# All gate and up pairs as seven-product jobs, with the norm's scale moved onto the gate

## The chip, the cores and the metric

The kernel runs on one core of one Trainium2 chip, as one launch. The metric is the device time of one execution in microseconds. The core's engines are named as in the profile: PE is TensorE's matmuls and PEld its weight loads, DVE is VectorE, ACT is ScalarE, POOL is GpSimd, SP is SyncE, which issues most of the DMA transfers. A name with a q (SPq, POOLq) is the queue of that engine.

## The reference, cut to what matters

A decoder of two layers computes one step for 512 prompt tokens and 32 sample tokens, 544 in all, in float32 with 1024 features. Each layer has a mixer (a short gated convolution in the first, retention with four heads in the second) and a gated feed-forward with 2816 hidden features:

```
x = x + mixer(rmsnorm(x, norm_mix))
x = x + (silu(h @ w_gate) * (h @ w_up)) @ w_down      with h = rmsnorm(x, norm_ffn)
rmsnorm(x, g) = x * rsqrt(mean(x*x over features) + 1e-6) * g
```

The scale `rsqrt(...)` is one number per token, the gain `g` one per feature. Since `h @ w` is linear, the scale of a token may be put on the result of the product instead of on its operand. That fact is used by both kernels, in different places.

## The kernel before, in words

Features lie on the 128 partitions and tokens along the free dimension. The residual x is eight tiles of 128 x 544 (x0 to x7). TensorE multiplies in a reduced float32 format, so each float32 operand is split into a high and a low part and each product is three matmuls: high by high, high by low, low by high. A matmul has 128 x 128 weights and 272 tokens, half of the 544. `split` (L184) makes the parts: ScalarE copies the high part (L185), VectorE subtracts it (L186). `split_adding` (L189) makes the low part in another way: ScalarE copies the negated high part and a DMA issued by GpSimd adds the source to it in memory (L193). Weights come as pieces of 128 x 1024 through three buffers (`wts`).

**The gate and up products.** The hidden features are 22 blocks of 128, taken as 11 pairs (m, m + 11). An ordinary pair takes 192 matmuls: a gate and an up piece for each of two blocks, each 8 feature tiles x 3 x 2 halves of the tokens (`project`, L164). A seven-product job does the gate (or the up) of a pair for both halves of the tokens as one 2 x 2 block product by seven multiplications in place of eight: 7 x 4 x 3 = 84 matmuls, so 168 for gate and up. It works on sums and differences: `weights7` (L407) makes those of the weights (four VectorE operations over 512 columns and four splits), `operands` (L397) those of x, once a layer, as seven operand tiles for each of four pairs of feature tiles (k, k + 4). The seven products accumulate in three PSUM banks; between products ScalarE copies a running sum out (a snapshot, L515) and VectorE adds it to others (L518). Class `Job` (L440) has the products as `begin`, `middle` and `end`; `run` (L490) puts the next job's beginning between the middle and the end of the one before.

**Before the change**, the first two pairs of each layer (`WHOLE = 2`) are ordinary ones (`whole_pairs`, L555). Their operands are x times the gain, split into `xh` and `xl` as the residual becomes final (`split_x`, L195); the norm's scale R goes onto their results. While they run, the sum of squares (`square_sum`, L205, with GpSimd adding, L215) becomes R (`rms_scale`: five one-column matmuls L244, a power on GpSimd L220, six small matmuls L224, a copy L256). Then `operand` (L546) makes the job operands as x times gain times R on VectorE. Jobs for the pairs 2 to 10 follow. After each three pairs `down` (L645) multiplies by w_down and adds to x (`residual`, L264).

**What stands ahead of the jobs.** In the first layer it is the convolution's output projection: eight blocks of 48 matmuls, one for each tile of x. In the second layer it is the last head's output projection (`out_project`, L1141): eight blocks of 24 matmuls, the first two interleaved.

**What sets the order.** The kernel is written with a tile framework that schedules the instructions itself: it orders each engine's queue from its own estimates of durations and inserts the waits. At run time each engine executes its queue strictly in that order. So the order in the text above is not always that on an engine.

## Time and profile before

| | us |
|---|---|
| runs shown | 1469.80, 1469.88, 1473.02 |
| their median | 1469.88 |
| the profiled execution, its own time | 1470.36 |
| its span in the profile | 1468.5 |
| TensorE busy in the span | 1457.3 |

The span runs from the first to the last recorded instruction of the profiled execution. Times in a timeline are from the start of the span. In a group's row stand the line, the engine, the operation, output and inputs by the program's names, the shape and the count; behind the bar the busy time and the mean duration of one in ns; and last the idle time of that engine ahead of them with what ended it. Matmuls overlap one another, so the sum of their durations is more than the time they take. In the rows of a stretch each engine's busy time is followed by its number of instructions.

### The profile page before, as it was taken

To read this page: it belongs to the slowest core of one execution; us is meant where nothing else is said; L and a number is where in the kernel's file an instruction comes from. 1 tells how busy PE (TensorE), PEld (TensorE's weight loads), DVE (VectorE), ACT (ScalarE), POOL (GpSimd) and SP (SyncE) were. 2 spreads that over 40 slices of the span, in tenths; PEclk is the share of its full clock that TensorE was granted. 3 is DMA by queue.
4 is the path that set the end of the run, shared out by engine and by line. 5 is a ranking of instruction groups with operands and counts; after the bars stand their busy time and mean duration, and the time that the engine had idled before them with its cause. 6 is when DMAs were issued, how large, how long until landed. Compare 5 with 4: busy or idle time off the path is not lost.

```text
span 1468.5 us, 26015 instructions
## 1 busy us (share of the span) xinstructions
PE 1457.3 (99%) x11016; PEld 1388.8 (95%) x11016; DVE 920.5 (63%) x1397; ACT 572.4 (39%) x821; POOL 84.3 (6%) x107
## 2 busy tenths in 40 slices
PE   9999999999999999999999999999999999999998
PEld 9999999999999999897987988898799999999997
DVE  6545439847748647648645934844759847748645
ACT  5222355625525434242142224114265625525424
POOL 0100220000000003000000000000030000000002
PEclk9999999999999999999999999999999999999999
DMA  6222274232322325336335613714564232332322
GB/s 226 86 87 87 89 179 109 91 100 90 102 94 87 101 65 181 116 115 232 100 115 173 202 49 121 264 42 143 173 158 108 91 105 87 104 92 93 101 65 83
DMA packets 69748, 172.83 MB, mean 118 GB/s; under 512 B 6512, under 2 KB 23792, under 8 KB 69632
## 3 DMA queue, kind: packets, MB, share of 16 engines
q1 hardware_dynamic: 66576, 162.01, 33.9%
q0 software_dynamic: 2192, 7.94, 3.3%
q8 instruction: 86, 1.41, 0.4%
q10 hardware_dynamic: 864, 1.22, 0.2%
q14 instruction: 30, 0.25, 0.1%
HBM read 149.97 MB, written 21.18 MB: 117 GB/s over the span
## 4 chain that ended last, share of the span: by engine, by line
PE 93%; DVE 4%; DMA 2%; POOL 1%; ACT 0%; issue 0%; DVEq 0%; POOLq 0%; ACTq 0%; SPq 0%
PE mm L172 41%; PE sm L458 26%; PE sm L172 13%; PE sm L906 2%; PE sm L907 2%; PE sm L908 2%; DMA S<-in_rets_dram 2%; DVE S L1138 1%; PE sm L160 1%; PE sm L162 1%; PE sm L161 1%; PE sm L1117 1%; PE mm L913 1%; DVE yn L1048 0%; DVE wl L186 0%
## 5 line engine op out<-in xcount | busy, mean ns | idle before, releaser
L185 ACT ACTIVATE wh<-w 128x1024 fp32r<-128x1024 f32 (+4 forms) x215 | 210.0, 980 | 448.2 <-PE mm L172 252.2
L186 DVE TENSOR_TENSOR wl<-w,wh 128x1024 fp32r<-128x1024 f32 (+4 forms) x215 | 243.1, 1134 | 44.3 <-ACT wh L185 40.9
L172 PE MATMUL mm<-xh,wh 128*128 128x272 f32 x1060 | 222.7, 291 | 0.0
L172 PE MATMUL mm<-xh,wl 128*128 128x272 f32 x1060 | 219.2, 289 | 0.0
L172 PE MATMUL mm<-xl,wh 128*128 128x272 f32 x1060 | 218.8, 288 | 0.0
L172 PEld LDWEIGHTS mm<-xh,wh 128*128 128x128 f32 x1060 | 166.5, 189 | 5.0 <-DVE wl L186 3.4
L458 PE MATMUL sm<-oh,wh 128*128 128x272 f32 x576 | 166.7, 289 | 0.0
L458 PE MATMUL sm<-oh,wl 128*128 128x272 f32 x576 | 166.6, 289 | 0.0
L172 PEld LDWEIGHTS mm<-xl,wh 128*128 128x128 f32 x1060 | 166.4, 189 | 0.0
L458 PE MATMUL sm<-ol,wh 128*128 128x272 f32 x576 | 166.3, 289 | 0.0
L172 PEld LDWEIGHTS mm<-xh,wl 128*128 128x128 f32 x1060 | 165.5, 189 | 0.4
L266 DVE TENSOR_TENSOR x<-x,mm 128x544 f32<-128x544 f32 x85 | 61.2, 720 | 144.8 <-PE mm L172 144.8
L458 PE MATMUL sm<-oh,l 128*128 128x272 f32 x432 | 124.9, 289 | 0.0
L458 PE MATMUL sm<-oh,h 128*128 128x272 f32 x432 | 124.8, 289 | 0.0
L458 PE MATMUL sm<-ol,h 128*128 128x272 f32 x432 | 124.8, 289 | 0.0
L458 PEld LDWEIGHTS sm<-oh,wh 128*128 128x128 f32 x576 | 108.7, 189 | 0.5 <-ACT u L515 0.4
L458 PEld LDWEIGHTS sm<-oh,wl 128*128 128x128 f32 x576 | 108.8, 189 | 0.0
L458 PEld LDWEIGHTS sm<-ol,wh 128*128 128x128 f32 x576 | 108.6, 188 | 0.0
L186 DVE TENSOR_TENSOR l<-w,h 128x1024 fp32r<-128x1024 f32 x72 | 68.8, 956 | 55.6 <-ACT h L185 55.4
L172 PE MATMUL mm<-xh,f 128*128 128x272 f32 x576 | 99.3, 288 | 0.0
L172 PE MATMUL sm<-xh,wh 128*128 128x272 f32 x412 | 88.4, 291 | 0.3 <-DVE rs L219 0.3
L172 PE MATMUL sm<-xh,wl 128*128 128x272 f32 x412 | 86.7, 288 | 0.0
(268 smaller groups left out, 2866.5 us busy)
## 6 DMA issues: line engine op xcount, KB each, us to landing
w<-in_ffgu_dram SPq DMA_DIRECT2D x88, 512.0 KB, 3.5
w<-in_ffdn_dram SPq DMA_DIRECT2D x96, 192.0 KB, 2.5
S<-in_rets_dram SPq DMA_DIRECT2D x16, 1024.0 KB, 7.9
out_rets_dram<-S SPq DMA_DIRECT2D x16, 1024.0 KB, 4.9
w<-in_cvin_dram SPq DMA_DIRECT2D x21, 512.0 KB, 3.5
w<-in_rtqk_dram SPq DMA_DIRECT2D x16, 512.0 KB, 3.8
w<-in_rtv_dram SPq DMA_DIRECT2D x16, 512.0 KB, 3.9
w<-in_rtg_dram SPq DMA_DIRECT2D x16, 512.0 KB, 4.1
```

The lines of the kernel that those rows point to most:

```text
L160: nc.tensor.matmul(out, lh, rh, start=start, stop=False, skip_group_check=True)
L161: nc.tensor.matmul(out, lh, rl, start=False, stop=False, skip_group_check=True)
L162: last_product[0] = nc.tensor.matmul(out, ll, rh, start=False, stop=stop, skip_group_check=True)
L172: last_product[0] = nc.tensor.matmul(half(pt, hf)[:, :HT], w[:, c], act[k][:, hf * HT : (hf + 1) * HT], start=(first and k == ks[0] and i ...
L185: h = nc.scalar.activation(dh, src, AF.Copy)
L186: nc.vector.tensor_sub(dl, src, dh.bitcast(F32))
L266: last_residual[0] = nc.vector.tensor_add(xk, xk, p)
L458: nc.tensor.matmul(out, w[:, c], b[k][:, at, :], start=(first and k == 0 and i == 0), stop=(k == n - 1 and i == 2), skip_group_check=True,)
L906: nc.tensor.matmul(out, xh[kt][:, ts_], wh[:, cw], start=(kt == 0), stop=False)
L907: nc.tensor.matmul(out, xh[kt][:, ts_], wl[:, cw], start=False, stop=False)
L908: nc.tensor.matmul(out, xl[kt][:, ts_], wh[:, cw], start=False, stop=(kt == KT - 1))
L913: nc.tensor.matmul(pvs[g * NS : (g + 1) * NS, 0, :], xs[:, kt, :], raw[kt // 2][:, kt % 2 * DV : (kt % 2 + 1) * DV], start=(c == 1), stop= ...
```

## The change

All eleven pairs of both layers become seven-product jobs; `whole_pairs` and `WHOLE` are gone.

- The job operands are made from x times the gain only (`operand`, on ScalarE instead of VectorE), so they don't wait for R. The loop that makes them takes the tiles of x in the order 0, 4, 1, 5, 2, 6, 3, 7 (`PAIRED`), and the two output projections ahead of the jobs finish x in an order to match. `split_x` with the feed-forward's gain is gone there.
- The gate's three blocks are collected unscaled; then the whole 128 x 1088 gate tile is multiplied by R, put through silu and multiplied by R again, the second time for the up product, which stays unscaled.
- The squares use the one tile `sqlast` in place of a pool of two; this holds at the beginning of the kernel too. The steps of R run between the products of the first job (`weave`).
- In `weights7` two of the four splits become `mixed`: the first 512 columns as before, the other 512 by the negated copy and an adding DMA from GpSimd.
- The memory pools of all stages are laid out anew, with `reuse_waits="tile"`: a new tile waits for the tiles whose place it takes, not for the whole pool before it.

```diff
-WHOLE = 2
+PAIRED = [0, 4, 1, 5, 2, 6, 3, 7]
...
-            sq = pool.tile([P, T], F32, tag=tag, name=nm("sq"), bufs=bufs)
+            sq = pool.tile([P, T], F32, tag=tag, name=nm("sq"), bufs=bufs) if pool else sqlast
...
-                    square_sum(kt, tp, add=nc.vector)
+                    square_sum(kt, None, add=nc.vector)
...
-        for n in range(KT):
+        wide("m")
+        for n in PAIRED:
             wh, wl = load_piece(a["cvout"][n], KT * P)
             pt = psum()
             project(pt, wh, wl, 0, yh, yl)
             residual(n, pt)
-            split_x(n, g_ffn(0, n))
-            square_sum(n, tp)
...
+    def mixed(wh, wl, w, src):
+
+        n = KP * P
+        nc.scalar.activation(wh, w, AF.Copy)
+        nc.vector.tensor_sub(wl[:, :n], w[:, :n], wh[:, :n].bitcast(F32))
+        nc.scalar.activation(wl[:, n:], wh[:, n:].bitcast(F32), AF.Copy, scale=-1.0)
+        nc.gpsimd.dma_start(wl[:, n:], src[:, n:], accum_op=ALU.add)
...
-        split(*p1, w1)
+        mixed(*p1, w1, src1)
...
-        split(*p3, w3)
+        mixed(*p3, w3, src2)
...
+                next(self.weave, None)
...
             def operand(k):
+
                 f = fp.tile([P, 5, HT], F32, tag="f", name=nm("f"))
                 for i in range(2):
-                    nc.vector.scalar_tensor_tensor(
-                        f[:, 2 * i : 2 * i + 2, :], halves(x[k + i * KP]), g_ffn(layer, k + i * KP), R,
-                        op0=ALU.mult, op1=ALU.mult,
+                    nc.scalar.activation(
+                        f[:, 2 * i : 2 * i + 2, :], halves(x[k + i * KP]), AF.Copy, scale=g_ffn(layer, k + i * KP)
                     )
                 operands(f, oh[k], ol[k])
-
-            def whole_pairs():
...
                 def gate(what, src):
                     g = tile2("g")
+                    r = R.rearrange("p a b -> p (a b)").unsqueeze(1).to_broadcast([P, 2, T])
                     if what == "c21":
-                        nc.scalar.activation(g[:, 1, :HT], src, AF.Silu)
-                    elif what == "c22":
-                        nc.scalar.activation(g[:, 1, HT:], g[:, 1, HT:], AF.Silu)
+                        nc.scalar.activation(g[:, 1, :HT], src, AF.Copy)
                     elif what == "c12":
-                        nc.scalar.activation(g[:, 0, :], g[:, 0, :], AF.Silu)
+                        nc.vector.tensor_mul(g, g, r)
+                        nc.scalar.activation(g, g, AF.Silu)
+                        nc.vector.tensor_mul(g, g, r)
...
-            wide("mmss")
-            whole = whole_pairs()
             wide("m")
+            for i, kt in enumerate(PAIRED):
+                if i % 2 == 0:
+                    operand(kt)
+                square_sum(kt, None, last=PAIRED[-1])
             groups = [list(range(m, min(m + GROUP, HJ))) for m in range(0, HJ, GROUP)]
-            jobs = [job for m in range(WHOLE, HJ) for job in gate_up(m)]
+            jobs = [job for m in range(HJ) for job in gate_up(m)]
...
-            run(jobs, inside, after)
+            steps = rms_scale()
+            run(jobs, after, steps)
+            drain(steps)
...
-            wide("mms")
-            for n2 in range(4):
+            wide("m" if rest else "mms")
+            for n2 in (0, 2, 1, 3):
...
-        for kt in range(KT):
-            split_x(kt, g_ffn(1, kt))
-            square_sum(kt, tp, f"rt{kt % 2}", 1)
-
     ffn(1, None)
```

More of the change, by code (lines that the diff above doesn't have):

```diff
@@ L272, in hybrid_decode_kernel @@
     with ExitStack() as c0:
-        tp = c0.enter_context(tc.tile_pool(name="cv", bufs=2))
-        one = c0.enter_context(tc.tile_pool(name="cv1", bufs=1))
+        low = c0.enter_context(tc.tile_pool(name="cv0", bufs=1, reuse_waits="tile"))
+        one = c0.enter_context(tc.tile_pool(name="cv1", bufs=1, reuse_waits="tile"))
+        tp = c0.enter_context(tc.tile_pool(name="cv", bufs=2, reuse_waits="tile"))
+        high = c0.enter_context(tc.tile_pool(name="cv2", bufs=1, side="right", reuse_waits="tile"))
         fs = one.tile([P, KT, NB, 6], F32, tag="fs", name="fs")
@@ L277, in hybrid_decode_kernel @@
         R2 = one.tile([P, 2, HT], F32, tag="R2", name="R2")
-        yh = [one.tile([P, T], F32R, tag=f"yh{k}", name=f"yh{k}") for k in range(KT)]
-        yl = [one.tile([P, T], F32R, tag=f"yl{k}", name=f"yl{k}") for k in range(KT)]
         st = one.tile([P, KT, NB, 2], F32, tag="st", name="st")
+        yhh = low.tile([P, KT, T], F32R, tag="yh", name="yh")
+        yll = high.tile([P, KT, T], F32R, tag="yl", name="yl")
+        yh, yl = [[t[:, k, :] for k in range(KT)] for t in (yhh, yll)]
         def start():
@@ L447, in hybrid_decode_kernel @@
         lead = False
+        weave = iter(())
         def prepare(self):
@@ L488, in end, with run @@
             self.take("c12", self.c)
-    def run(jobs, inside, after):
+    def run(jobs, after, steps):
         jobs[0].lead = True
@@ L494, in run @@
         jobs[0].begin()
+        jobs[0].weave = steps
         for i, job in enumerate(jobs):
@@ L499, in run @@
             job.middle()
-            inside(i)
             if nxt is not None:
```

77 lines of the change are left out of this document (20 added, 57 removed).

## The prediction

> **What bounds the kernel now.** I read the page first, then the busy time by stretches, then the timelines around the places where the new jobs begin, and last the groups by shape for durations.
>
> ```profile
> PE 1457.3 (99%) x11016; PEld 1388.8 (95%) x11016; DVE 920.5 (63%) x1397; ACT 572.4 (39%) x821; POOL 84.3 (6%) x107
> PEclk9999999999999999999999999999999999999999
> PE 93%; DVE 4%; DMA 2%; POOL 1%; ACT 0%; issue 0%; DVEq 0%; POOLq 0%; ACTq 0%; SPq 0%
> ```
>
> TensorE is busy 1457.3 of 1468.5 us at the full clock, and the chain that ended last runs 93% through it. So the time is the number of matmuls times their pace, plus idle gaps. The pace isn't the listed duration, because matmuls overlap. It comes from a full stretch (columns: stretch, its length, then busy us and instructions of PE, PEld, DVE, ACT, POOL):
>
> ```profile
> 340.00:380.00 40.00, 40.00 (x320) 40.00 (x319) 32.99 (x50) 23.39 (x36) 0.00 (x0) 1.00 0.29 99
> 440.00:460.00 20.00, 20.00 (x161) 20.00 (x161) 16.61 (x25) 11.59 (x19) 0.00 (x0) 1.00 0.28 85
> ```
>
> 320 matmuls in 40.00 us are 0.125 us each. In the second stretch, inside the seven-product jobs, VectorE is busy 83% and ScalarE 58%. One job (84 matmuls) lasts 10.5 us, a pair of jobs 21.
>
> **What is removed.** An ordinary pair of gate and up pieces costs 4 pieces x 48 = 192 matmuls, as two jobs it costs 2 x 84 = 168. Two pairs in each of two layers: 4 x 24 = 96 fewer, and the changed program's instruction list has exactly 96 fewer 128x272 matmuls, with every other TensorE form unchanged. 96 x 0.125 = **12.0 us**, 6.0 in each layer. All of it is on the path.
>
> **What covered the start of the jobs.** In the second layer the last retention product, the ordinary pairs and the first job stand like this:
>
> ```profile
> 1082.30 0.42 PE L172 MATMUL mm<-yh,wl 128*128 128x272 f32 x2
> 1082.55 0.42 PE L172 MATMUL mm<-xh,wh 128*128 128x272 f32 x2
> 1132.86 0.29 PE L458 MATMUL sm<-oh,wh 128*128 128x272 f32 x1
> ```
>
> The ordinary pairs fill 1082.55 to 1132.86, 50.3 us in which the norm's scale, the four job operands and the first job's weights are made. Afterwards the jobs begin right at 1082.55. That cover goes, and the question is what is late. The prices:
>
> ```profile
> L185 ACT ACTIVATE wh<-w 128x1024 fp32r<-128x1024 f32 x166 | 175.4, 1060 | 372.8 <-PE mm L172 197.9 <-PE sm L172 112.7 <-issue 29.5
> L185 ACT ACTIVATE h<-w 128x512 fp32r<-128x512 f32 x36 | 22.8, 632 | 4.3 <-PE sm L458 3.6
> L197 ACT ACTIVATE xh<-x,vec 128x544 fp32r<-128x544 f32 x31 | 22.8, 746 | 8.4 <-DVE x L266 7.3 <-DMA x<-in_xT_dram 1.0
> L214 ACT ACTIVATE sq<-x 128x544 f32<-128x544 f32 x28 | 18.0, 648 | 0.8 <-DVE x L266 0.5 <-DVE sqacc L215 0.3
> L185 ACT ACTIVATE oh<-f 128x1360 fp32r<-128x1360 f32 x8 | 10.7, 1334 | 3.2 <-DVE f L401 3.0
> L185 ACT ACTIVATE oh<-f 128x544 fp32r<-128x544 f32 x8 | 5.1, 657 | 9.4 <-DVE f L404 9.4
> L588 ACT ACT_TABLE_LOAD x1 | 1.3, 1283 | 0.8 <-DVE gu L586 0.8
> ```
>
> ```profile
> L186 DVE TENSOR_TENSOR l<-w,h 128x1024 fp32r<-128x1024 f32 x36 | 44.1, 1225 | 55.4 <-ACT h L185 55.4
> L418 DVE TENSOR_TENSOR w<-w,w 128x512 f32<-128x512 f32 x36 | 24.8, 688 | 0.6
> L266 DVE TENSOR_TENSOR x<-x,mm 128x544 f32<-128x544 f32 x85 | 61.2, 720 | 144.8 <-PE mm L172 144.8
> L186 DVE TENSOR_TENSOR ol<-f,oh 128x1360 fp32r<-128x1360 f32 x8 | 12.4, 1571 | 0.0
> ```
>
> ```profile
> L215 POOL TENSOR_TENSOR sqacc<-sqacc,sq 128x544 f32<-128x544 f32 x22 | 34.4, 1564 | 702.6 <-ACT sq L214 702.6
> L220 POOL TENSOR_TENSOR rs<-rs,expo 128x1 f32<-128x1 f32 x20 | 12.6, 632 | 457.6 <-DVE mv L1045 378.3 <-DVE rs L219 79.3
> L193 POOL DMA_DIRECT2D wl<-in_ffgu_dram x13 | 11.3, 870 | 47.4 <-ACT wl L192 42.9 <-ACT R L256 4.5
> ```
>
> **Second layer.** Time is counted from the end of the last output product (1082.55). The residuals of x0, x1, x4, x5, x2, x3, x6, x7 come at the ends of eight blocks. Six blocks of 24 matmuls (3.0 us each) follow the first two, so x0 is final at about -18.6 and x7 at about +0.9. In the changed program ScalarE has, between x0 and the high part of the third operand: 6 scaled copies, 6 squares, 4 copies of 1024 columns, 3 of 512, 3 of 1360, 2 of 544. That is 4.48 + 3.89 + 4.24 + 1.89 + 4.00 + 1.31 = 19.8 us. Consecutive ones start a little before the listed end:
>
> ```profile
> 451.11 0.64 ACT L185 ACTIVATE xh<-u 128x544 fp32r<-128x544 f32 x1
> 451.66 0.63 ACT L185 ACTIVATE h<-w 128x512 fp32r<-128x512 f32 x1
> ```
>
> 0.55 apart for 0.64, so 24 x 0.09 = 2.2 comes off: 17.6. Waits are added: 1.35 for x4, x6 and a freed weight buffer, and 2.8 for GpSimd. The squares now share one tile, so each waits until GpSimd has added the one before (1.56), and between two adds GpSimd issues a DMA (0.87). 17.6 + 4.15 = 21.75 from -18.6, so the third operand is ready at +3.15. TensorE's order, fixed when the program is built, puts 13 matmuls of the first two operands there (1.6 us), then waits: 1.5 us idle. The fourth operand's high part comes after a square, two scaled copies, another square, a 1024 copy, a 544 and the 1360: +8.55. TensorE's own work up to that point is 29 matmuls and five one-column sums:
>
> ```profile
> L244 PE MATMUL sm<-cb,sqacc x30: 164/209/251, 207.2 to 1093.2; 128*128 128x1 f32 x30
> ```
>
> 3.6 + about 0.7 = 4.3 us. So it has lost 8.55 - 4.3 = 4.2 us by then, the 1.5 included. Behind it come the low part (1.57 on VectorE against 1.4 of matmuls, 0.2), the power on GpSimd for the norm (0.63 plus its neighbours, 0.3), and the next job's second weight tile, of which there is one buffer: its copy can begin only when TensorE has read the old one, and TensorE's next product and a snapshot behind another 1024 copy wait too (1.4). Sum for this layer: **+6.1 us**, against the 6.0 saved.
>
> **First layer.** There a block has 48 matmuls (6.0 us), so ScalarE keeps up and three operands stand ready before the last block ends. 27 matmuls of them and the sums run while the fourth is made. Chain after the end: residual 0.2 + 0.72, scaled copy, square (1.2 until both have left, behind a 1024 copy), add 0.72: sum ready at 3.25 against 24 matmuls = 3.0, idle 0.25. Then eps and power 1.1 against 5 matmuls, 0.5. Later the one buffer of the second weight tile, 1.06 for its copy, nothing beside it, and 0.7 in four small waits, among them the table load of 1.28 before the first gate function. **+2.5 us**, between 1 and 4.
>
> **Beginning of the kernel.** Squares and VectorE's adds alternate there through one tile instead of two (0.65 + 0.72 each, seven times); the five sums stand 40 matmuls later in TensorE's order, which takes up nearly all: +0.3.
>
> **Steady jobs.** VectorE loses half of two 1024 subtractions per job (4 x 0.54 per pair) and gains two multiplications over 1088 columns per pair (by the 1024 row and its pace about 1.2 each): -2.16 + 2.4, so it stays at 84%. ScalarE gains 4 negated copies of 512 and a longer gate function, 11.6 to about 14 of 21 us. GpSimd and its queue get 88 transfers of 256 KB instead of 15 of 512 KB. Cost taken: 0, because the filled halves have time:
>
> ```profile
> wl<-in_ffgu_dram POOLq DMA_DIRECT2D x13, 512.0 KB, 6.4
> ```
>
> Copy, negated copy and issue are 1.06 + 0.63 + 0.87 = 2.6 us after a buffer is free, and TensorE reads the half 110 matmuls (13.8 us) after that. Landing may take 11 us, and twice the size took 6.4. From below: no gain is possible here, since TensorE was already full. From above: see the second rival.
>
> **The sum.** The profiled execution took 1470.36 us (span 1468.5 and 1.9 around it). 1470.36 - 12.0 + 6.1 + 2.5 + 0.3 = 1467.3. It lies 0.5 over the median of 1469.88, so on the median's footing 1466.8; I say **1467.0 us**, 0.2% under. About 0.3% (4.4 us) is what a measurement of this kernel can tell from no change.
>
> **Rivals.**
>
> 1. *The starts are covered after all.* The order that I read was made by a scheduler that puts the third operand 13 matmuls after the end; if its durations hold, the lists above are too long (GpSimd's adds are the softest: rows there run from 1.4 to 1.8). Then only the first layer's power and the single weight buffer remain, some 3 us in all: 1470 - 12 + 3 = 1461. Against it: the sum of ScalarE's list doesn't depend on order. Chance 0.22.
>
> 2. *ScalarE's snapshot comes late in every job (slower).* In a job, the accumulating bank must be copied between two products with only one product, 12 matmuls or 1.5 us, between them.
>
> ```profile
> 445.55 1.06 ACT L185 ACTIVATE wh<-w 128x1024 fp32r<-128x1024 f32 x1 [0.38 <-PE sm L458]
> 447.19 0.40 ACT L515 ACTIVATE u<-sm 128x272 f32<-128x272 f32 x1 [0.58 <-PE sm L458]
> 448.70 0.40 ACT L515 ACTIVATE g<-sm 128x272 f32<-128x272 f32 x1 [1.11 <-PE sm L458]
> ```
>
> The idle 0.58 ahead of the snapshot at 447.19 is just where the new negated copy of 0.63 goes. The snapshot needs 0.40 of 1.5, so it decides from 1.0 us of lateness on. Every further 0.25 us costs 44 x 0.25 = 11 us: 1478. For it: ScalarE and VectorE are queues in fixed order, and a late DMA or VectorE step passes on. Against: 1.0 us of room. Chance 0.14.
>
> 3. *The gaps of the second layer run together and the clock falls.* What the trace has is one gap of 1.16 us, with the clock at 1.00 after it:
>
> ```profile
> 1056.00:1060.00 4.00, 2.83 (x18) 2.39 (x19) 3.18 (x9) 1.39 (x4) 0.72 (x1) 1.00 0.05 20
> 1056.95 0.52 PE L172 MATMUL mm<-yh,wh 128*128 128x272 f32 x2 [1.16 <-ACT yh L185]
> ```
>
> The expected gaps are 1.5 us and less, with matmuls between. If the 4.2 us became one gap and the next stretch of that length ran at half pace, 4 us more would be lost: 1471. Chance 0.06. [...]
>
> The case of the sum itself has the remaining 0.58, from 1464.5 to 1471.
>
> **The numbers.** Faster by over 0.3% (under 1465.5): rival 1 and the low edge of the main case, 0.22 + 0.06 = 0.28. Slower by over 0.3% (over 1474.3): rival 2 and 0.01 of rival 3, 0.15. Within: 0.57. The range 1461 to 1474 leaves out the lower half of rival 1 and nearly all of rival 2.
>
> **What would show it.** Right: 96 fewer matmuls at 0.125; in the second layer idle TensorE of about 6 us within 25 us of the last output product, put down to the operands' copies (ACT, L186) and weight copies (L414); 2 to 3 us in the first layer; no idle time in the later jobs. Wrong: waits at L471 spread over all jobs for snapshots (L529) or for GpSimd's transfers, or a granted clock under 1.00. If the second layer's idle is under 2 us, my walk through ScalarE's list is what failed.

## The result and the profile after

The changed kernel is slower: 1476.32 us against 1471.14 on the same chip (medians of eight executions each), ratio 1.0034 with a 95% interval of 1.0023 to 1.0045. That is 5.2 us, just over the 0.3% that can be told from no change, and 9 us above the forecast of 1467.0.

The page of the changed kernel, its lines of engines, granted clock and chain, and the row of its core:

```profile
PE 1453.5 (98%) x10920; PEld 1381.1 (94%) x10920; DVE 963.4 (65%) x1472; ACT 627.8 (43%) x914; POOL 150.5 (10%) x180
PEclk9999999999999999999999999999989999999999
PE 88%; DVE 6%; DMA 1%; ACT 1%; POOL 1%; issue 1%; SPq 0%; DVEq 0%; POOLq 0%; ACTq 0%
...
core 0: 1475.8 us, clock 0.992
```

The 96 matmuls are gone (11016 to 10920), yet the span grew by 7.3 us. The line of the granted clock, all nines before, has one 8, and the chain runs 88% through TensorE instead of 93%: there are now places where it waits for others.

**Where the time went.** Four rows of the changed kernel's timeline mark the two stages that the change touches: the last output product, and the first product with w_down, in either layer.

```profile
201.38 0.41 PE L173 MATMUL mm<-yh,wl 128*128 128x272 f32 x2
...
296.91 0.42 PE L173 MATMUL mm<-xh,wh 128*128 128x272 f32 x2
...
1084.22 0.42 PE L173 MATMUL mm<-yh,wl 128*128 128x272 f32 x2
...
1183.46 0.42 PE L173 MATMUL mm<-xh,wh 128*128 128x272 f32 x2
```

From the end of the first to the start of the second are 95.1 us, in the second layer 98.8 us. In the kernel before the same marks lie 94.0 us apart in either layer; the last of them:

```profile
1176.75 0.42 PE L172 MATMUL mm<-xh,wh 128*128 128x272 f32 x2
```

The profiled executions, cut at these marks and, in the first layer, at the last job's end:

| stretch, us | before | after | difference | predicted |
|---|---|---|---|---|
| up to the first start | 200.6 | 201.8 | +1.2 | +0.3 |
| first layer, first three pairs | 94.0 | 95.1 | +1.1 | -6.0 + 2.5 |
| the rest of its jobs | 255.8 | 254.8 | -1.0 | 0 |
| its last w_down group and the second layer's mixer | 532.3 | 532.9 | +0.6 | 0 |
| second layer, first three pairs | 94.0 | 98.8 | +4.8 | -6.0 + 6.1 |
| the rest | 291.8 | 292.3 | +0.6 | 0 |

The two starts account for 9.3 of the 10.4 us between forecast and measurement. The last row is -1.2 in the jobs and +1.8 behind the last output transfer.

**The clock.** Stretches of the changed kernel around the two starts (stretch, length, busy us and instructions of PE, PEld, DVE, ACT, POOL, granted clock, DMA share, GB/s):

```profile
204.00:208.00 4.00, 3.10 (x22) 2.59 (x20) 2.57 (x5) 2.49 (x4) 0.90 (x1) 0.88 0.37 131
208.00:212.00 4.00, 2.39 (x12) 2.39 (x12) 1.38 (x3) 0.00 (x0) 2.43 (x2) 0.50 0.24 27
212.00:216.00 4.00, 4.00 (x26) 3.89 (x26) 1.12 (x3) 2.80 (x5) 0.00 (x0) 0.77 0.26 43
...
1084.00:1088.00 4.00, 2.26 (x19) 2.04 (x17) 4.00 (x9) 3.26 (x6) 1.91 (x2) 1.00 0.40 66
1088.00:1092.00 4.00, 2.39 (x13) 2.18 (x14) 4.00 (x4) 2.63 (x4) 3.23 (x2) 0.88 0.35 131
1092.00:1096.00 4.00, 2.76 (x14) 2.44 (x12) 4.00 (x9) 3.90 (x5) 0.02 (x1) 0.50 0.00 0
1096.00:1100.00 4.00, 4.00 (x19) 4.00 (x19) 2.26 (x4) 0.35 (x2) 2.25 (x2) 0.50 0.73 167
1100.00:1104.00 4.00, 4.00 (x29) 3.83 (x27) 0.89 (x2) 1.58 (x4) 0.00 (x0) 0.84 0.19 34
```

At the clock of 0.50 the products start 0.227 us apart, in place of 0.125 (twelve such steps from 1096.92 to 1099.64): in the stretch from 1096 TensorE never idles, and only 19 matmuls run where 32 would. The time at half clock follows from the column: (0.12 + 0.50 + 0.23) x 8 = 6.8 us at the first start, (0.12 + 0.50 + 0.50 + 0.16) x 8 = 10.2 us at the second. Both are multiples of 3.4, and half of it is lost where TensorE has work: up to 3.4 and 5.1 us. I call this half pace. The profiled execution of the kernel before shows none at its starts.

**The waits.** TensorE's waits in the changed kernel between 1075 and 1110 us (what waited, for which line; us in all, times, longest):

```profile
PE sm L471 <- ACT oh L186: 2.5, 1, 2.5
PE sm L471 <- ACT wh L414: 1.2, 1, 1.2
PE sm L471 <- DVE ol L187: 0.9, 1, 0.9
PE mm L173 <- DVE x L267: 0.7, 1, 0.7
```

The predicted 6.1 us at the second start were to be waits for operand and weight copies. These are there, 2.5 + 1.2 + 0.9 and 0.8 more in two small ones, 5.4 us in all; the last row, 0.7, lies ahead of the last output product and so before this stage. At the first start the timeline has this:

```profile
205.57 1.25 PE L245 MATMUL mm<-cb,sqacc 128*128 128x1 f32 x10 [0.78 <-DVE sqacc L212]
...
207.10 2.46 POOL L221 TENSOR_TENSOR rN<-rN,expo 128x5 f32<-128x5 f32 x1 [3.21 <-DVE rN L220]
...
209.61 2.77 PE L225 MATMUL mm<-cb,rN 128*128 128x128 f32 x12 [1.74 <-POOL rN L221]
```

The power for the norm took 2.46 us, and the matmuls that spread its result (L225) stand five products behind the sums in TensorE's order: a wait of 1.74 us. But the clock falls at 207.0 (the stretch from 204 has 0.12 x 8 = 0.96 us at half clock), ahead of that wait: behind the 0.78 us that the sums waited and the 1.1 us of their one-column matmuls.

**The steady jobs** are as fast as before, at least:

```profile
340.00:380.00 40.00, 40.00 (x322) 40.00 (x321) 34.81 (x56) 26.86 (x42) 6.62 (x8) 1.00 0.62 147
440.00:460.00 20.00, 20.00 (x163) 20.00 (x162) 17.34 (x28) 14.22 (x22) 2.79 (x4) 1.00 0.65 152
```

ScalarE went from 11.59 to 14.22 of 20 us and VectorE from 16.61 to 17.34, and TensorE has no gap.

### The profile page after: what moved, and what is told of

Same layout as the page of the kernel before. It is cut to its first block, busy times and chain, and to the rows that moved or that the text cites. A ratio compares the mean times of both kernels' runs of the same rounds, so it can differ in the third digit from the quotient of the medians.

```text
span 1475.8 us, 26203 instructions
## 1 busy us (share of the span) xinstructions
PE 1453.5 (98%) x10920; PEld 1381.1 (94%) x10920; DVE 963.4 (65%) x1472; ACT 627.8 (43%) x914; POOL 150.5 (10%) x180
## 4 chain that ended last, share of the span: by engine, by line
PE 88%; DVE 6%; DMA 1%; ACT 1%; POOL 1%; issue 1%; SPq 0%; DVEq 0%; POOLq 0%; ACTq 0%
PE mm L173 35%; PE sm L471 31%; PE sm L173 8%; PE sm L883 2%; PE sm L884 2%; PE sm L885 2%; PE sm L161 1%; PE sm L163 1%; PE sm L162 1%; DVE S L1115 1%; PE sm L1094 1%; DVE wl L187 1%; DMA w<-in_ffgu_dram 1%; DVE ol L187 1%; DMA S<-in_rets_dram 1%
## 5 line engine op out<-in xcount | busy, mean ns | idle before, releaser
L186 ACT ACTIVATE wh<-w 128x1024 fp32r<-128x1024 f32 (+4 forms) x142 | 132.7, 939 | 369.4 <-PE mm L173 222.4
L471 PE MATMUL sm<-oh,wh 128*128 128x272 f32 x704 | 204.6, 291 | 4.1 <-ACT oh L186 2.5
L471 PE MATMUL sm<-ol,wh 128*128 128x272 f32 x704 | 203.7, 290 | 0.9 <-DVE ol L187 0.9
L471 PE MATMUL sm<-oh,wl 128*128 128x272 f32 x704 | 203.6, 289 | 0.0
L173 PE MATMUL mm<-xh,wh 128*128 128x272 f32 x932 | 195.0, 290 | 0.2 <-ACT wh L186 0.2
L187 DVE TENSOR_TENSOR wl<-w,wh 128x1024 fp32r<-128x1024 f32 (+4 forms) x142 | 153.9, 1088 | 28.5 <-ACT wh L186 26.3
L471 PE MATMUL sm<-oh,h 128*128 128x272 f32 x528 | 152.5, 289 | 1.3 <-ACT h L186 0.9
L417 POOL DMA_DIRECT2D wl<-in_ffgu_dram x88 | 76.6, 871 | 595.9 <-ACT wl L416 359.4
L414 ACT ACTIVATE wh<-w 128x1024 fp32r<-128x1024 f32 x88 | 93.2, 1059 | 70.7 <-PE sm L471 47.0
L471 PEld LDWEIGHTS sm<-oh,h 128*128 128x128 f32 x528 | 100.1, 190 | 1.8 <-ACT h L186 1.7
```

The source lines that it names most:

```text
L173: last_product[0] = nc.tensor.matmul(half(pt, hf)[:, :HT], w[:, c], act[k][:, hf * HT : (hf + 1) * HT], start=(first and k == ks[0] and i ...
L186: h = nc.scalar.activation(dh, src, AF.Copy)
L187: nc.vector.tensor_sub(dl, src, dh.bitcast(F32))
L414: nc.scalar.activation(wh, w, AF.Copy)
L417: nc.gpsimd.dma_start(wl[:, n:], src[:, n:], accum_op=ALU.add)
L471: nc.tensor.matmul(out, w[:, c], b[k][:, at, :], start=(first and k == 0 and i == 0), stop=(k == n - 1 and i == 2), skip_group_check=True,)
```

## The experiments

Three theories for the starts. **Half pace**: gaps of about 2 us drop the clock, and that is the price. **Operands**: ScalarE, VectorE and GpSimd make the operands later than I reckoned, through the squares and their sum. **Halves by DMA**: the two mixed splits and their 88 transfers cost the time. All numbers follow in one table: medians in us, the ratio to the kernel before on the same chip, the two stages of the profiled execution with the half pace in each, and the time from the last output transfer to the end of the span. The medians are over all executions, the stages and the half pace from one.

| kernel | median | before | ratio [95%] | first stage | half pace | second stage | half pace | end |
|---|---|---|---|---|---|---|---|---|
| before | | | | 94.0 | 0 | 94.0 | 0 | 4.0 |
| after | 1476.32 | 1471.14 | 1.0034 [1.0023, 1.0045] | 95.1 | 6.8 | 98.8 | 10.2 | 5.8 |
| e1_filled | 1474.12 | 1471.60 | 1.0017 [1.0008, 1.0026] | 90.3 | 0 | 98.8 | 3.4 | 5.7 |
| e2_squares_late | 1484.70 | 1471.60 | 1.0089 [1.0072, 1.0106] | 99.8 | 10.2 | 102.4 | 10.2 | 5.7 |
| e3_adds_on_vector | 1476.39 | 1471.60 | 1.0034 [1.0021, 1.0047] | 95.0 | 6.8 | 97.5 | 10.2 | 5.5 |
| e4_two_squares | 1470.77 | 1471.60 | 0.9995 [0.9986, 1.0005] | 95.0 | 6.8 | 91.9 | 0 | 5.5 |
| e5_square_tiles | 1486.86 | 1471.74 | 1.0107 [1.0090, 1.0124] | 99.4 | 10.2 | 102.8 | 17.1 | 5.4 |
| e6_later_spreads | 1473.09 | 1471.74 | 1.0008 [0.9998, 1.0017] | 90.4 | 0 | 98.7 | 10.2 | 5.8 |
| e7_plain_split | 1480.64 | 1471.74 | 1.0063 [1.0048, 1.0078] | 98.0 | 6.8 | 99.1 | 10.2 | 4.1 |
| e8_second_old | 1469.94 | 1471.74 | 0.9989 [0.9979, 0.9998] | 92.1 | 3.4 | 94.4 | 0 | 5.3 |
| e9_vector_later | 1470.30 | 1470.97 | 0.9993 [0.9984, 1.0003] | 89.8 | 0 | 96.6 | 10.2 | 5.5 |
| e10_and_fillers | 1468.75 | 1470.97 | 0.9983 [0.9974, 0.9992] | 89.8 | 0 | 95.2 | 3.4 | 5.5 |
| e11_squares_lag | 1473.84 | 1470.97 | 1.0009 [0.9996, 1.0022] | 96.2 | 10.2 | 94.3 | 0 | 5.4 |
| e13_combined | 1465.60 | 1470.24 | 0.9969 [0.9957, 0.9981] | 89.8 | 0 | 92.4 | 0 | 5.5 |

Of the times expected below, those of e6, e8 and e13 came within 0.4 us of their theory A. Those of e1, e3, e4, e9 and e10 fell between the two that were given, and e2 and e5 were slower than any. e7 has theory B's time with theory A's end, and e11 lies in theory B's range, but through its first layer.

### Matmuls of ones in the gaps

```diff
+                if which == 1 and self.fills.get(k):
+                    fill(self.fills[k], self.bank, last_job[0])
...
+            jobs[0].fills = ({}, {2: 8, 3: 7})[layer]
+            steps = rms_scale(fills=(6, 0)[layer])
```

`fill` issues that many matmuls of 128 columns of ones, in the second layer ahead of the third and fourth operand's products and in the first ahead of the spreads. Each starts an accumulation anew in the bank where the product ahead is being summed, and partial products are missing from this kernel's output. In e10 and later the fillers have a bank of their own.

> The changed kernel with 8 and 7 matmuls of ones put into TensorE's order at the second layer's start (ahead of the third and the fourth operand) and 6 ahead of the norm's spreads in the first layer; they compute nothing that is used. Theory A (half pace): in the changed kernel's profile the clock falls to 0.50 at both starts, and some 70 matmuls at 0.23 instead of 0.125 us, with the sums and spreads at the same pace, cost about 2.7 + 4.4 = 7 us on top of the waits. The fillers keep the clock at 1.00 and the time falls from 1476.3 to 1469 to 1471. Theory B (waits alone): TensorE would wait for ScalarE's and VectorE's operands just the same, a faster pace only makes the waits longer: clock up, time 1475 to 1477.

The first stage falls by 4.8 us to 90.3 with no half pace, which is the 94.0 - 6.0 + 2.5 = 90.5 of the prediction. The second stage stays at 98.8, although its half pace falls from 10.2 to 3.4 us. ScalarE's timeline says why:

```profile
1088.39 0.66 ACT L211 ACTIVATE sqlast<-x 128x544 f32<-128x544 f32 x1 [1.30 <-POOL sqacc L216]
1088.96 1.04 ACT L416 ACTIVATE wh<-w 128x1024 fp32r<-128x1024 f32 x1
1089.90 1.87 ACT L186 ACTIVATE oh<-f 128x544 fp32r<-128x544 f32 x2
```

The fourth operand's high part is ready at 1091.8, 10.8 us after the end of the last output product (1080.97), as in the changed kernel (1093.56 + 1.87 - 1084.63 = 10.8). TensorE still waits 4.6 us in this stage (5.4 in the changed kernel), and the fillers themselves take 1.95 and 1.72 us of it. So at the first start half pace, with the wait that the fillers replace, is the whole loss against the forecast; at the second it lay beside an operand chain that is late in any case.

### The squares

Four edits on the chain of squares. First, all squares behind the last operand's high part (`last_high`):

```diff
-            for i, kt in enumerate(PAIRED):
-                if i % 2 == 0:
-                    operand(kt)
-                square_sum(kt, None, last=PAIRED[-1])
+            for kt in PAIRED[::2]:
+                operand(kt)
+            with tc.issue_after(last_high[0].ins):
+                for kt in PAIRED:
+                    square_sum(kt, None, last=PAIRED[-1])
```

> The changed kernel with ScalarE's eight squares of each start queued behind the high part of the last operand, so that the sums and the norm come about 100 matmuls later. Theory A (the squares and their adds delay the operands): six squares of 0.65 us and the waits for GpSimd's adds leave the list ahead of the fourth operand in the second layer; it comes 4 us or more earlier, the waits of 6 us at the second start fall under 3 and the clock stays up: 1465 to 1469. Theory B (weights and operands alone fill ScalarE and VectorE): the fourth operand moves by less than 2 us: 1474 to 1477. A third way: the adds come too slowly through the one tile, and the sums make TensorE wait later for it: 1473 to 1480.

Second, GpSimd's adds on VectorE:

```diff
-                square_sum(kt, None, last=PAIRED[-1])
+                square_sum(kt, None, last=PAIRED[-1], add=nc.vector)
```

> The changed kernel with the six middle adds of the squares at each start on VectorE instead of GpSimd. Theory A (the two engines stretch one another: GpSimd's adds take 1.4 to 2.5 us, and VectorE's 272-column subtractions beside them 1.6 instead of 0.43): adds at 0.72, no stretched VectorE rows, ScalarE no longer waits for GpSimd between squares, 1470 to 1473. Theory B (VectorE is full at the second start, 4.0 of 4.0 us in six slices in a row): six adds more make its low parts later still, 1477 to 1480.

Third, six of the eight squares and their adds left out:

```diff
-                square_sum(kt, None, last=PAIRED[-1])
+                if i in (0, 7):
+                    square_sum(kt, None, last=PAIRED[-1])
```

> The changed kernel with only the first and the last of the eight squares at each start; the other six squares and their adds are left out, so the norm is taken over two of eight tiles. It bounds what the squares cost: theory A (squares and adds delay the operands) 1464 to 1468, with the second start's waits under 3 us; theory B (weights and operands alone fill the engines) 1474 to 1477.

Fourth, squares in four tiles of the gate's pool instead of the shared one:

```diff
-                square_sum(kt, None, last=PAIRED[-1])
+                square_sum(kt, tp, "gu", 4, last=PAIRED[-1])
```

> The changed kernel with the six middle squares of each start in four tiles of the gate's pool instead of the one shared tile, so that ScalarE need not wait for GpSimd's add before the next square. Theory A (that wait is in the chain): in the second layer ScalarE sat idle 2.08, 1.59 and 1.29 us ahead of squares, put down to the adds; the fourth operand comes 2 to 4 us earlier: 1471 to 1474. Theory B (ScalarE's order was made round those holes, and the squares' own 0.65 us and the copies are the chain): 1475 to 1477.

**e4** takes the second stage to 91.9 with no half pace, 6.9 us less; the fourth operand comes at +6.2 instead of +10.8. So the operands are late through the squares. **e3** shows that a part of that isn't worth the same part of the price: the operand comes at +7.4, 3.4 us earlier, the stage is only 1.3 us shorter. Its timeline still has a wait of 2.59 us, and the 10.2 us of half pace are still there; a stretch of it, with 19 matmuls in 4 us as in the changed kernel:

```profile
1097.00:1101.00 4.00, 4.00 (x19) 4.00 (x19) 2.57 (x6) 1.86 (x3) 2.09 (x2) 0.50 0.35 99
```

So either cause covers the other: with less half pace (e1) the operand is waited for, with the operand earlier (e3) the clock is down.

**e2** made the operands early (+5.9), but then TensorE waited for the sums (1.8 us) and for snapshots behind the squares, and half pace came back in three pieces: putting the work off moves the gap. **e5** is inconclusive for the shared tile. The gate's tiles came free late, and the squares bunched ahead of the last operand. It shows something else, in the timelines of GpSimd and VectorE:

```profile
1090.24 12.35 POOL L216 TENSOR_TENSOR sqacc<-sqacc,sq 128x544 f32<-128x544 f32 x6 [3.70 <-ACT sq L215]
...
1096.90 4.49 DVE L187 TENSOR_TENSOR ol<-f,oh 128x544 fp32r<-128x544 f32 x2
```

While GpSimd adds without a break (2.06 us each), two of VectorE's subtractions, of 544 and 1360 columns, take 4.49 us together. In e13, with the adds on VectorE itself, a pair of the same two forms takes 2.20.

### The spreads behind more products

```diff
-        for _ in range(4):
+        for _ in range(room):
...
-            steps = rms_scale()
+            steps = rms_scale(room=12)
```

> The changed kernel with the norm's spreads 30 matmuls behind its sums in TensorE's order instead of 5; no fillers. Run e1_filled took 4.9 us off the first layer's stage from its first job matmul to its first down matmul (95.3 to 90.4) and nothing off the second's (99.0). Theory A (the wait of 1.74 us for the power stands right behind sums that hardly use the array, and the half pace follows from it): without that wait the first stage comes to 90 to 92 us and the time to 1471 to 1473. Theory B (only the fillers kept the clock up; the wait for the fourth operand's low part takes the place): stage 94 to 95, time 1475 to 1477.

The spreads now stand 30 matmuls behind the sums instead of five. In the stretches of this kernel, the one from 206 holds the power (GpSimd's 2.07 of 4 us):

```profile
206.00:210.00 4.00, 3.60 (x30) 3.63 (x31) 2.50 (x5) 1.51 (x2) 2.07 (x1) 1.00 0.43 135
...
210.00:214.00 4.00, 3.77 (x31) 3.45 (x29) 2.05 (x4) 3.24 (x6) 2.12 (x3) 1.00 0.36 63
```

No wait for the power, clock 1.00, first stage 90.4: 4.7 us less, as with the fillers, with nothing added. That is 1.7 for the wait and about 3 for the two pieces of half pace. The second piece had the wait to set it off. The first had begun ahead of it. The sums of e6 wait too (0.62 us) and bring no piece here; e8, below, has it, and the last experiment says why.

### The halves by DMA

```diff
-        mixed(*p1, w1, src1)
+        split(*p1, w1)
...
-        mixed(*p3, w3, src2)
+        split(*p3, w3)
```

> The changed kernel with its mixed splits (negated copy on ScalarE, GpSimd's accumulating transfer) made plain: the low part whole on VectorE. Theory A (the mixed splits cost nothing in the steady jobs; but their 88 transfers lengthen what lies between the last output transfer's issue and the end, 4.0 us in the kernel before, 5.6 to 5.8 in the changed one and in four variants of it): that stretch back to about 4.0, jobs at the same pace, starts within 2 us: 1472 to 1476. Theory B (VectorE needs the relief: 88 subtractions of 0.54 us more would be on the path): jobs over 21.2 us a pair and 1480 or more; the end's stretch unchanged.

Slower by 4.3 us than the changed kernel: the mixed halves pay. In the profiled executions 2.9 us of this lie in the first stage and only 0.9 in the later jobs of both layers; why the first start needs them isn't tested. But one thing goes back to the old value, the end. The last output transfers from SP's queue in the kernel before, the changed one and this one (transfers' ns shortest, median, longest; first and last):

```profile
L749 SPq DMA_DIRECT2D out_yT_dram<-yb x2: 332/338/344, 1461.3 to 1464.5; - x2
```

```profile
L725 SPq DMA_DIRECT2D out_yT_dram<-yb x2: 333/338/344, 1466.9 to 1470.0; - x2
```

```profile
L725 SPq DMA_DIRECT2D out_yT_dram<-yb x2: 332/338/343, 1471.8 to 1474.9; - x2
```

To the ends of the spans (1468.5, 1475.8, 1479.0) it is 4.0, 5.8 and 4.1 us; every kernel of the table with the mixed halves has 5.3 to 5.8. So the 88 transfers issued by GpSimd cost 1.2 to 1.7 us behind the last output, though in the changed kernel the last of them is issued at 1424.5; what happens there the profile doesn't show.

### The second layer's old start

The first layer as in e6, and in the second layer the two ordinary pairs of the kernel before:

```diff
+            def whole_pairs():
...
+                if layer == 1:
+                    nc.vector.scalar_tensor_tensor(
```

> The first layer as in run e6_later_spreads (all pairs as jobs), the second layer's start as in the kernel before (two pairs in ordinary products), new pools and mixed splits throughout. Theory A (each start pays for itself, the stages add up): first stage 90 to 92 us (94.2 before), second 94 to 95 (99.0 in the changed kernel), end 1.7 us longer, kernel beginning 1.2 later: 1466 to 1470, ahead of both. Theory B (the new pools, not the starts, cost the time): 1473 to 1477.

94.4 us for the second stage, as before the change, no half pace, and 1469.94 in all: the new start costs the second layer 4.4 us, seen from the other side. In the first layer, with e6's order, one piece of half pace is back and the stage 1.7 us longer. The timeline and the stretches of this kernel there:

```profile
205.59 1.25 PE L246 MATMUL mm<-cb,sqacc 128*128 128x1 f32 x10 [0.75 <-DVE sqacc L213]
```

```profile
204.00:208.00 4.00, 3.25 (x26) 3.07 (x26) 2.57 (x5) 2.50 (x4) 0.88 (x1) 0.94 0.42 135
208.00:212.00 4.00, 4.00 (x23) 4.00 (x23) 1.84 (x4) 1.26 (x2) 2.44 (x2) 0.63 0.25 26
```

(0.06 + 0.37) x 8 = 3.4 us, without any wait for the power: the 0.75 us ahead of the sums and their own 1.1 us were enough. Where VectorE adds and the sums don't wait at all (e9, e10, e13), that piece never came.

### Putting the parts together

e9 is e3 and e6 in one; e10 adds nine fillers ahead of the fourth operand in the second layer, in a bank of their own; e11 has six, and each square comes one pair of tiles later:

```diff
-                square_sum(kt, None, last=PAIRED[-1])
+                if i >= 2:
+                    square_sum(PAIRED[i - 2], None, add=nc.vector)
+            with tc.issue_after(last_high[0].ins):
+                for kt in PAIRED[-2:]:
+                    square_sum(kt, None, last=PAIRED[-1], add=nc.vector)
```

Expected of e9:

> Runs e3_adds_on_vector and e6_later_spreads in one: the middle adds of the starts on VectorE, the spreads 30 matmuls behind the sums. It is the control of run e10_and_fillers. If the stages add up: kernel to the first layer's stage 202 to 203 us, first stage 90.4, second 97.5 (operands 3.4 us earlier than in the changed kernel, but the half pace still there), 1471 to 1472. If the later spreads also help the second stage, 1469.

Expected of e10:

> Run e9_vector_later with 9 matmuls of ones just ahead of the second layer's fourth operand, where run e3_adds_on_vector idled 2.59 us and then ran 8 us at 0.23 us a matmul with all operands made. They write a bank of their own and compute nothing that is used. Theory A (half pace is a price of its own wherever the operands are there): clock 1.00 throughout, second stage 97.5 to 93, time 4 to 5 us under run e9, 1466 to 1468. Theory B (the waits are all, as run e1_filled's second stage of 98.8 with fillers seems to say): second stage 97 to 98, time that of e9.

Expected of e11:

> Run e10_and_fillers with each pair of squares behind the next pair's operand on ScalarE, the last two behind the last operand (6 fillers). Theory A (operands first: two squares of 0.65 us less ahead of the fourth operand, the sums late but not waited for): second stage 91 to 92.5, the bound that run e4_two_squares set, time 1464 to 1466. Theory B (as in run e2_squares_late the sums and the snapshots behind late squares cost more than the operand gains): 1470 to 1476.

The adds on VectorE, worth 1.3 us by themselves, are worth 2.1 beside e6's second stage (98.7 to 96.6). e10 removes two of three pieces of half pace (10.2 to 3.4 us), and the stage is 1.4 us shorter; the nine fillers themselves take some of TensorE's time (six of them took 1.26 us in e1, from 206.70 to 207.96). e11 is two results in one. In the second layer the operand comes at +5.5 and the stage is 94.3 without half pace, a wait of 1.6 us for the power left. In the first layer, where ScalarE had kept up, the same edit brings 10.2 us of half pace and 96.2 us. So e13 takes e9's first layer, e11's second, and the spreads 27 matmuls behind the sums:

```diff
+            with tc.issue_after(last_job[0].ins) if room == 18 else ExitStack():
+                spread(half(pt, hf)[:, at : at + hi - lo], tt, lo, hi)
...
+            steps = rms_scale(pt=early, room=(12, 18)[layer])
```

> First layer as in run e9_vector_later, second as in run e11_squares_lag (squares a pair behind, adds on VectorE, 6 fillers), with the second layer's spreads forced 27 matmuls behind the sums instead of 12. Theory A (the stages add up and the wait of 1.6 us for the power goes): kernel up to the first stage 202.3, first stage 89.8, second 92.5 to 93, the rest as measured (254.8, 532.5, 254.8, 31.8, 5.5): span 1464.3 and 1466 us, ahead of both kernels. Theory B (another wait, snapshots or weights, takes its place): second stage 94 to 95, 1468.

```profile
1084.00:1088.00 4.00, 2.80 (x16) 2.17 (x16) 4.00 (x8) 2.31 (x5) 0.86 (x1) 1.00 0.71 185
1088.00:1092.00 4.00, 3.91 (x30) 3.70 (x31) 4.00 (x8) 2.67 (x5) 0.00 (x0) 1.00 0.09 16
1092.00:1096.00 4.00, 4.00 (x33) 3.96 (x33) 3.50 (x8) 2.44 (x6) 2.55 (x2) 1.00 0.70 199
```

These stretches of e13 begin 5.8 us after its last output product: 79 matmuls in 12 us at clock 1.00. In the changed kernel the 12 us at the same distance, 1090.5 to 1102.5, hold 54. The stage is 92.4 us, 6.4 less than in the changed kernel. In all 1465.60, ratio 0.9969 [0.9957, 0.9981], 4.6 us below the kernel before, where the changed kernel was 5.2 above. That lies between the forecast (1467.0) and the first rival (starts covered, 1461).

### How long a wait drops the clock

The kernel before, with pauses put into full stretches of w_down products: TensorE waits for a chain of GpSimd adds of chosen width (columns in `PAUSES`), everything else being computed as before.

```diff
+PAUSES = (((64,), (544,), (272, 544)), ((272,), (544, 544), (544,)))
...
+                nc.gpsimd.tensor_tensor(sqlast[:, :w], src[:, :w], src[:, :w], op=ALU.add)
...
+            last_pause[0] = nc.tensor.matmul(out, ones, sqlast[:, 0:1], start=True, stop=True, skip_group_check=True)
```

> The kernel before with one pause of TensorE in each of six down groups, where it is otherwise full: the sixth block waits for a GpSimd chain that begins with the fifth block's residual (64, 544, 272 then 544 columns in the first layer, 272, 544 twice, 544 in the second). By the rows that makes idle times of about 1.5, 2.7, 3.4, 1.9, 4.2 and 2.7 us, 16.4 in all. Theory A (what the changed kernel shows: waits of 1.74 and 2.45 us end the full pace): behind pauses of about 2 us and more, most often, 3 to 7 us at 0.50, that is 1.5 to 3.5 us more each; 1488 plus 5 to 14. [...]

One execution took 1495.53 us, in theory A's range. Its timeline, the three pauses of the first layer, and its stretches around the first two, cut where the clock changes:

```profile
319.37 0.38 PE L170 MATMUL mm<-sqlast,ones 128*128 128x1 f32 x2 [1.83 <-POOL sqlast L168]
...
423.67 0.38 PE L170 MATMUL mm<-sqlast,ones 128*128 128x1 f32 x2 [2.70 <-POOL sqlast L168]
...
527.54 0.38 PE L170 MATMUL mm<-sqlast,ones 128*128 128x1 f32 x2 [3.75 <-POOL sqlast L168]
```

```profile
316.30:319.71 3.41, 1.58 (x13) 1.36 (x13) 2.13 (x3) 0.84 (x1) 0.93 (x1) 1.00 0.24 94
319.71:323.13 3.42, 3.42 (x17) 3.42 (x17) 0.47 (x2) 0.00 (x0) 0.00 (x0) 0.50 0.49 158
323.13:326.54 3.41, 3.41 (x29) 3.41 (x29) 1.57 (x3) 0.84 (x1) 0.00 (x0) 1.00 0.00 0
...
418.70:422.11 3.41, 2.27 (x19) 2.06 (x17) 1.03 (x2) 0.84 (x1) 0.23 (x1) 1.00 0.40 154
422.11:425.53 3.42, 1.86 (x15) 1.86 (x16) 2.06 (x2) 0.00 (x0) 1.51 (x1) 1.00 0.45 151
425.53:428.94 3.41, 3.41 (x30) 3.41 (x29) 1.50 (x3) 0.46 (x1) 0.00 (x0) 1.00 0.01 2
```

Behind the wait of 1.83 us the clock fell to 0.50 for one stretch of 3.41 us; behind the longer one of 2.70 us it did not; behind 3.75 it did. In the second layer it stayed behind 2.18 and 2.70 and fell behind 4.20. The same with twelve pauses of two widths:

```diff
-PAUSES = (((64,), (544,), (272, 544)), ((272,), (544, 544), (544,)))
+PAUSES = (((64,),) * 3, ((544,),) * 3)
...
-                        if ms[-1] < HJ - 1 and n == 5:
+                        if ms[-1] < HJ - 1 and n in (2, 6):
```

> The kernel before with twelve pauses of TensorE of run e12_pauses' kind: two in each of three down groups of each layer, those of the first layer with 64 columns (1.8 us there), those of the second with 544 (2.7 us). Theory A (length decides): all six of one layer fall to half pace or none; by e12's 1.83, with a fall, and 2.70, without, that already failed once. Theory B (the moment decides, as for a clock that looks at stretches of time of its own): some of the six of each length fall, each fall followed by some 3.6 us at 0.25 us and more a matmul. Theory C (only waits of 3.4 us and more fall and the 1.83 was a single case): none of the twelve.

The clock fell behind three of six waits of 1.83 to 1.90 us and behind five of six of 2.63 to 2.70 us, as theory B has it. Over both kernels: 4 of 7 at 1.8 to 1.9, 5 of 9 at 2.2 to 2.7, 2 of 2 above 3.7. The total of e14 (1518.21) isn't used: its order of instructions costs other things too. So the clock fell behind one of two waits of the same length and not behind the other, and 1.83 us was enough where the moment was bad.

The traces show what the moment was. In the changed kernel the granted clock is 0.50 from 207.02 to 213.85 and from 1091.08 to 1101.32 us: 6.83 and 10.24 us, two and three steps of 3.413 us, and the two falls are 259 such steps apart, to 0.01. In e12 the falls at 319.71, 527.93 and 1319.82 are 61 and 232 steps apart, and the other profiles with more than one fall fit the same step as closely as their stretches tell, to about 0.04. Drawn through these times, a grid of such steps cuts a pause into parts. Take as its hole the time from the end of the last full product ahead of it to the start of the next, the pause's own matmuls included. In the 11 pauses of both kernels behind which the clock fell, the largest part of the hole within one step was 1.93 us or more; in the 7 others, 1.89 or less. The hole of 2.08 us at 317.54 lies within one step. The one of 2.9 us at 420.97 is cut into 1.14 and 1.81, and the clock stays. The starts fit nearly: the sums' hole (their wait and their matmuls) is 1.89 us within one step in the changed kernel and 1.86 in e8, both with a fall, and 1.73 in e6, cut in two, without. So in these 18 pauses and three starts about 1.9 us without full products within one step of 3.41 parts the cases with a fall from those without. This is read from the traces afterwards, not forecast and tested.

It fits that the same kernel gets more or fewer pieces from one execution to the next. The eight of the changed kernel go from 1474.54 us at a mean granted clock of 0.995 to 1477.94 at 0.992 (the profiled one has 0.992), so a stage time in the tables can be some 3 us shorter or longer in another execution. Those of e11 form two groups: three at 0.998 and 0.999 with 1469.04 to 1469.18 us, seven at 0.994 to 0.996 with 1472.72 to 1475.25.

## Why the prediction was wrong, point by point

- **The 96 matmuls**: right, 11016 to 10920. In e13, where TensorE waits about 1 us at the first start and 1.5 at the second, 4.6 of the 12.0 us show in the time.
- **Steady jobs at 0**: right on the safe side. The later jobs took 1.0 and 1.2 us less in the two layers; e7, with plain halves, gives back 0.6 in the first layer and 0.3 in the second. The second rival, late snapshots in every job, did not happen: clock 1.00 and TensorE full from 340 to 380.
- **The second start at 6.1**: wrong by 4.7, and this is the larger failed step. The waits that I listed came, most of them for the lines that I named, 5.4 us in all. What failed is that the sum had no term for half pace, and the third rival was given 0.06 and a condition, one gap of 4 us or more. Gaps of 2.5, 0.9 and 1.2 us with matmuls between them gave three pieces, 10.2 us at half clock, up to 5.1 us lost. They did run together, but not into one gap: the stretch from 1087.66 to 1091.08, the last before the fall, holds 1.05 us of the first gap and the 0.90 of the second. Nor was a gap of 4 us needed: in e12 the clock fell behind a single wait of 1.83. That the half pace would last as long as the gap, 4.2 us, was my estimate, which no run shows; it came in pieces of 3.41 us. And the gap of 1.16 us with the clock at 1.00 behind it, on which I had judged this rival, was luck: in e1 the same gap stands at 1053.27, and from 1055.12 on the clock is at 0.50 for 3.41 us.
- **The third operand at +3.15 and the fourth at +8.55**: they came at +4.0 and +10.8. I had taken 2.8 us in all for GpSimd, at 1.56 an add. The group in the changed kernel has 1728 ns each:

```profile
L216 POOL TENSOR_TENSOR sqacc<-sqacc,sqlast 128x544 f32<-128x544 f32 x12 | 20.7, 1728 | 49.0 <-ACT sqlast L215 49.0
```

and around the start they range from 1.35 to 2.50. ScalarE, VectorE and GpSimd in the changed kernel's timeline:

```profile
1077.91 0.66 ACT L215 ACTIVATE sqlast<-x 128x544 f32<-128x544 f32 x1 [2.08 <-POOL sqacc L216]
...
1080.16 0.66 ACT L215 ACTIVATE sqlast<-x 128x544 f32<-128x544 f32 x1 [1.59 <-POOL sqacc L216]
...
1089.53 2.49 POOL L216 TENSOR_TENSOR sqacc<-sqacc,sqlast 128x544 f32<-128x544 f32 x1 [0.77 <-ACT sqlast L215]
...
1090.75 1.57 DVE L404 TENSOR_TENSOR f<-f 128x272 f32<-128x272 f32 x1
...
1092.25 0.43 DVE L407 TENSOR_TENSOR f<-f 128x272 f32<-128x272 f32 x1
```

ScalarE waits 2.08 and 1.59 us for the shared tile, and VectorE's 272 columns take 1.57 us while GpSimd's add runs (to 1092.02) and 0.43 after it. The late operands and the half pace can't be priced apart: they hide each other (e1: 0, e3: 1.3, both with the lag in e13: 6.4).
- **The first start at 2.5**: the size failed, 7.1 came. For eps and power I took 1.1 us, from rows of 128x1; the power over 128x5 took 2.46. The kernel before has a row of that very shape, with a mean of 1.50 us, and the forecast didn't use it:

```profile
L220 POOL TENSOR_TENSOR rN<-rN,expo 128x5 f32<-128x5 f32 x3 | 4.5, 1498 | 14.2 <-DVE rN L219 14.2
```

I had taken 0.5 us of idle time for it, with the rest hidden behind five matmuls; it was 1.74, and the sums' wait was 0.78 in place of 0.25. And 6.8 us of half pace came that I didn't price, one piece from the sums' own hole and one with this wait. Without them (e1, e6) the stage is the predicted one within 0.2 us, but partly by luck: in e6 the sums wait 0.62 us and the power nothing.
- **The end**: +1.8, not in the sum. I looked at what the transfers cost in the jobs, not at what their number costs after the last one.
- **The beginning and the mixer**: +1.2 for +0.3, and +0.6 for nothing. In the mixer's end TensorE waits 0.69 us for the residual of an output block in the new order (the last row of the waits). What makes up the rest of the two was only read, not tested.

By the prediction's own marks, the granted clock under 1.00 was the sign of its failure, and the waits put down to L186 and L414 the sign that its walk through the queues named the right waits, though the fourth operand came 2.2 us later.

## What to carry to other kernels

Where a change takes away work that covered a transition, price the gaps that it leaves twice, as waits and as half pace, and remove both, since either alone hides the other. Here gaps that added up to about 1.9 us within 3.4 were enough for a piece of 3.4 us, up to 1.7 us lost each, and one trace without a fall proves little, since the moment decides. A small result that takes a slow engine 2.5 us belongs 20 matmuls or more (2.5 / 0.125) behind its inputs in TensorE's order; here that was worth 4.7 us at the first start. And cut the profile into stages before and after: a sum of small terms hides that two of them carry all the error.

## What was not expected of the hardware

- The time at half clock came as 3.4, 6.8, 10.2 and 17.1 us at the starts of these kernels, in steps of 3.413 us on one grid in each profile with more than one fall, and in e12 it followed a wait of 1.83 us and not one of 2.70. One-column matmuls didn't keep the clock up in e8: it fell behind a wait of 0.75 us with 1.1 us of them after it.
- GpSimd's adds over 128x544 and VectorE's operations were longer side by side, now one and now the other: in the changed kernel an add took 2.50 us at 1075.38, with VectorE busy, and 1.36 at 193.94, with VectorE mostly idle. VectorE's 272 columns took 1.57 us during an add and 0.43 after it, and its 512 columns 1.88 and 1.56 during the adds of 1.47 and 1.35 at 1078.66 and 1080.89, against 0.68 at 1074.49, without one.
- The end of the span, from the last output transfer on, takes 4.0 us with 15 adding transfers issued by GpSimd, 4.1 with none, and 5.3 to 5.8 with 87 or 88.
